# Moving 32 DRAM-to-DRAM transfers inside GpSimd's queue, and reordering the loads of one stage's entry

## The chip, the cores and the metric

The kernel runs on one core of a Trainium2 chip. The metric is device time in microseconds (us) of one execution. The engines are TensorE (PE, with its weight loads as PEld), VectorE (DVE), ScalarE (ACT) and GpSimd (POOL); SyncE (SP) only issues DMA transfers. Each engine works through its own list of instructions strictly in order, and waits at an instruction until the semaphores named there have their values. Transfers issued by SP and by GpSimd go through two queues that share the same 16 DMA engines.

## The reference

One inference step of a one-layer encoder for 544 rows (512 of a new stream, 32 of a running one), width 2048, all in fp32. The parts that matter here, cut from it:

```python
h = layer_norm(x, ln_in_g, ln_in_b)                       # x: 544 x 2048
proj = h @ w_in                                           # 2048 x 4928
hq, hf, hi, hg, cq, ckv, kr = jnp.split(proj, SPLITS, axis=-1)
o_h = hgrn2_recurrence(...)                               # 8 heads of 128
o_a = mla_attention(...)                                  # 8 heads of 128
mix = jnp.concatenate([o_h, o_a], axis=-1) @ w_out        # 2048 x 2048
h = layer_norm(ALPHA * h + mix, ln1_g, ln1_b)
ff = (silu(causal_conv3(h @ w_up)) * (h @ w_gate)) @ w_down
y = layer_norm(ALPHA * h + ff, ln2_g, ln2_b)
```

## The kernel before, in words

Activations lie transposed in SBUF: 128 features on the partitions, the 544 rows along the free axis, cut into two halves of 272 (`NI`). Every fp32 product is three matmuls: operands and weights are split into a rounded high part (`wh`, `aH`, made by ACT) and the rest (`wl`, `aL`, made by DVE as a difference), and PE multiplies high by high, low by high and high by low.

The stages, in order of time:

1. **Entry (0 to some 120 us).** SP loads the input in five row tiles (128 rows each, the fifth with the 32 rows), each as two halves, with `ident`, `par` (all small parameters) and the first eight weight blocks of 512 KB between them. For each row tile DVE takes statistics (`L277`, `L279`), GpSimd makes the factor of the norm in two tiny operations (`rs`, `L280` and `L281`, the second a power of -1/2), DVE normalises (`L287`), PE transposes (`tp`, `L297`), ACT applies the affine part and rounds (`L303`, `L304`), DVE makes the low part (`L305`). PE multiplies the first projection in `cq_half`, first for the rows of the first half, then for the second.
2. **Attention (to some 360 us).** Four pairs of heads: `proj_pair` projects and rotates a pair while `attend` works on the one before. The rotation needs the halves of each head exchanged: four SBUF copies `t<-t` on SP (`swapped`, L457 and L458), then GpSimd multiplies by the cosine (`L462`) and DVE by the sine (`L463`). `tick()` is called at every step of the projections.
3. **Recurrence (to some 790 us).** For each head two groups of weights go through a seven-product scheme (`Divided`): a 2x2 block matrix is multiplied with seven products of sums of blocks. The sums of weight blocks are made in SBUF by DVE and by accumulating transfers on GpSimd: `L782` (12 += 22, in `form`) and `L795` (11 += 21, in `low`; `form_next()` stands in the code behind it). `L994` is a tiny power on GpSimd in each head's `finish`.
4. **Block stage (790 to 945 us).** The output projection. Its first columns run with plain weights (`step`, `split_next`), and the norm's first sums are taken (`Norm.first`: `n_cb`, a copy on ACT, `L1139`). Then 28 products of the seven-product scheme (`Product`, PE `L1792`) for four column groups. Their weights come from DRAM: some are blocks of `w_out`, the others are sums of blocks. The sums of operands (`su`, tiles `us`) come from `sm_dr`, and `split_su` splits them on ACT and DVE (`L1416`, `L1417`). `out_sink` (DVE, `L1820` and `L1823`) adds a product's PSUM tile to the rows `zt`.
5. **Feed-forward and second norm (to the end).**

The **weight sums** of the block stage are the subject of the change. `forming(phase)` yields 32 transfers within DRAM on GpSimd's queue, 512 KB each, in six phases: eight plain copies of a block into its place (`wf_dr`), eight transfers that accumulate another block onto it, four copies of a sum, four accumulates, four copies, four accumulates. `form_next(n)` issues the next one if more than `n` are left. In the program text it is called from `tick()` in the attention stage, and from `low()` in the recurrence.

What sets the order: PE, DVE and ACT of the entry, and all engines of the recurrence's core and of the block stage, keep the order of the program text (`manual_schedule`). Elsewhere, for GpSimd and SP above all, a list scheduler places an instruction as early as its inputs allow by its own estimate. The weight sums have no input but DRAM weights, so it puts them at the head of GpSimd's list, among the first operations of the kernel, however late `form_next` stands in the text.

Of the kernel before, what the change touches and what calls it, by code (L numbers as in the profile page):

```python
# [11 lines left out]
ALU = mybir.AluOpType  # L12
# [47 lines left out]
def tile_encoder_step(ctx, tc, xp, xs, w_in, w_in4, w_kr, w_q_b, w_kv_b, w_out, w_out4, w_up, w_gate, w_down, w_down2,  # L60
# [33 lines left out]

    def form_next(n=0):
        if len(forms) > n:
            forms.pop(0)()

    par = const.tile([P, N_PAR], F32, name="par")
    ident = const.tile([P, P], F32, name="ident")  # L100
# [299 lines left out]
    with tc.tile_pool(name="mp", bufs=1) as mp, tc.tile_pool(name="psa", bufs=4, space=PSUM) as psa:  # L400
# [274 lines left out]

        def tick():
            ticks[0] += 1
            if ticks[0] % 7 == 0:
                form_next(12)

        weave([proj_pair(0)], [], 0.0, tick)
        weave([proj_pair(1)], [attend(0)], 2.0, tick)
        weave([proj_pair(2)], [attend(1)], 2.0, tick)
        weave([proj_pair(3)], [attend(2)], 2.0, tick)
        weave([head_ig(0)], [attend(3)], 2.0, tick)
        while len(forms) > 12:
            form_next()

    def out_piece(kk, g):
# [13 lines left out]
    with tc.tile_pool(name="gp", bufs=1) as gp, tc.tile_pool(name="psg", bufs=1, space=PSUM) as psg:  # L703
# [60 lines left out]
        class Divided:  # L764
# [26 lines left out]
            def low(self, wh):  # L791
                wl = wp.tile([P, 1024], R, name="wl", tag="wl")
                V.tensor_tensor(out=wl, in0=self.t(self.key), in1=wh.bitcast(F32), op=ALU.subtract)  # L793
                if self.name == "s2":
                    G.dma_start(self.t("11"), self.src("21"), accum_op=ALU.add)  # L795
                    form_next()
                elif self.name not in ("11", "s1"):
                    slots.append(self.raw.pop(self.key)[0])
                    supply()
                return wh, wl  # L800
# [610 lines left out]
    def load_su(n, i):  # L1411
        G.dma_start(su[n][i][:, 1].bitcast(F32), sm_dr[i][:, ("s1", "s2", "s4").index(n)])

    def split_su(n, i):
        h, l = su[n][i][:, 0], su[n][i][:, 1]
        A.activation(h, l.bitcast(F32), AF.Copy)  # L1416
        V.tensor_tensor(out=l, in0=l.bitcast(F32), in1=h.bitcast(F32), op=ALU.subtract)  # L1417
# [14 lines left out]
    def joined(k, j, ps, eng=V):  # L1432
        z = zt[k][:, H_[j]]
        V.tensor_tensor(out=z, in0=z, in1=ps, op=ALU.add)
        nrm[j].add(zt[k], eng)
# [31 lines left out]
    def step(outs, w, j, kk):  # L1467
        for t in range(2):
            for k in range(4):
                kg = CAT_ORDER[4 * kk + k]  # L1470
                mm3([(outs[t], j)], (w[0][:, kg % 4], w[1][:, kg % 4]), (t * P, t * P + P), cact(kg),
                    kk == 0 and k == 0, kk == 3 and k == 3)
# [3 lines left out]
    with tc.manual_schedule():  # L1476
        order56 = [(kk, g) for g in (5, 6) for kk in ko]
        raws56, ws56 = [], []

        def raw_next():  # L1480
            if len(raws56) < 8:
                kk, g = order56[len(raws56)]
                raws56.append(load_raw(w_out[kk, g - 4], 4, 256))

        def split_next():
            ws56.append(split_w(raws56[len(ws56)], 4, 256))
            raw_next()

        for _ in range(3):
            raw_next()  # L1490
        for k in (0, 1, 2, 4, 6):
            G.dma_start(zt[k], h0_dr[k])
        for k in (10, 11, 12, 13, 8):
            dma(zt[k], h0_dr[k])
        for k in (3, 5, 7):
            G.dma_start(zt[k], h0_dr[k])
        for n in ("s1", "s2"):
            for i in range(2):
                load_su(n, i)
        split_next()  # L1500
        split_next()
        firsts = []
        for j in range(2):
            for t in range(2):
                z = zt[t][:, H_[j]]
                V.scalar_tensor_tensor(out=z, in0=z, scalar=ALPHA, in1=wo_tiles[t][:, PS_[j]], op0=ALU.mult, op1=ALU.add)
            firsts.append(nrm[j].first(zt[0], zt[1], early[0][:, 512 * j:512 * j + 512]))
            next(firsts[j])

        def next_firsts():  # L1510
            for f in firsts:
                next(f, None)

        five, six = pair_half(early[1], 0), pair_half(main_tile(), 0)
        step(five, ws56[0], 0, 0)
        split_next()
        next_firsts()
        step(five, ws56[1], 0, 1)
        split_next()
        next_firsts()  # L1520
        for i in range(2):
            load_su("s4", i)
        step(five, ws56[2], 0, 2)
        next_firsts()
        split_next()
        shifted(10, 0)
        shifted(11, 0)
        step(five, ws56[3], 0, 3)
        split_next()
        for k in range(HK):  # L1530
            load_21(k, d3_dr[k // 2][:, k % 2])
        step(six, ws56[4], 0, 0)
        split_next()
        for t in range(2):
            joined(10 + t, 0, five[t], G)
        step(six, ws56[5], 0, 1)
        split_next()
        shifted(12, 0)
        shifted(13, 0)
# [255 lines left out]
    with tc.manual_schedule():  # L1795
# [59 lines left out]
        def restore():  # L1855
            for k in range(HK):
                load_21(k, cat_dr[4 + k // 2][:, k % 2, NI:])

        NO = len(oitems)
        ohooks = {0: [lambda: split_su("s1", 1)], 1: [lambda: split_su("s2", 0)], 2: [lambda: split_su("s2", 1)],  # L1860
                  3: [lambda: split_su("s4", 0)], 4: [lambda: split_su("s4", 1)], 5: [lambda: split_21(range(4))],
                  6: [lambda: split_21(range(4, 8))],
                  NO - 2: [lambda: split_seventh(0)],
# [5 lines left out]
        oitems[0].prep()  # L1869
        step(six, ws56[7], 0, 3)  # L1870
        oitems[1].prep()
        split_su("s1", 0)
        for t in range(2):
            joined(12 + t, 0, six[t], G)
        play(oitems, 0, ohooks)
        restore()
        for n in (2, 3):
# [756 lines left out]
```

## Time and profile before

| | us |
|---|---|
| median of 3 runs | 2414.26 (2410.18 to 2414.37) |
| profiled execution | 2413.28 |
| its span | 2410.8 |
| PE busy | 2301.5 (95% of the span) |
| DVE busy | 1716.4 (71%) |
| ACT busy | 1096.8 (45%) |
| GpSimd busy | 272.6 (11%) |

The page also has the span in 40 equal slices of 60 us, the busy share in tenths. The first two slices differ from all others:

```profile
PE   2499999999999999999999999999999999999997
PEclk8699999999999999999999999999999999999998
```

In the time lines each row gives the start in us, the duration, engine, line, operation, output and inputs with their shapes, and in brackets the time the engine had stood idle and what released it. A name like `wf3s<-in_w_out` is output and input; buffer numbers are left out. "issue" as a releaser means that the profile shows nothing that was waited for.

### The profile page before, as it was taken

How to read it: one execution, taken by the hardware profiler on the slowest of the kernel's cores; microseconds unless marked ns; L12 is line 12 of the kernel's file. 1: busy time of each engine (PE TensorE's matmuls, PEld its weight loads, DVE VectorE, ACT ScalarE, POOL GpSimd, SP SyncE). 2: the span in 40 equal slices, each digit the busy share in tenths (PEclk: the TensorE clock that was granted, in tenths of full speed). 3: DMA queues.
4: the chain of work that ended last, by engine and by line, in shares of the span. 5: the costliest groups of instructions: out<-in, count | busy, mean ns of one | idle time of the engine just before them, and what ended most of it. 6: DMA issues, size and time to landing. Idle time of an engine off the chain costs nothing.

```text
span 2410.8 us, 44619 instructions
## 1 busy us (share of the span) xinstructions
PE 2301.5 (95%) x18244; PEld 2284.0 (95%) x18244; DVE 1716.4 (71%) x2395; ACT 1096.8 (45%) x1686; POOL 272.6 (11%) x343
## 2 busy tenths in 40 slices
PE   2499999999999999999999999999999999999997
PEld 1499999999999899999999999999999999999996
DVE  2344657777767578897777777777777777777776
ACT  2144543433445345665555555555555433333323
POOL 2201100100000211010100001010000111111102
PEclk8699999999999999999999999999999999999998
DMA  9753226555556854668677677767677998889832
GB/s 288 174 135 104 91 71 201 160 138 128 134 133 194 289 173 160 224 172 263 169 220 192 183 213 181 223 167 227 183 192 206 343 333 286 263 287 306 288 104 76
DMA packets 175772, 474.55 MB, mean 197 GB/s; under 512 B 16080, under 2 KB 80336, under 8 KB 168144
## 3 DMA queue, kind: packets, MB, share of 16 engines
q1 hardware_dynamic: 140112, 316.57, 38.3%
q0 software_dynamic: 35456, 155.14, 27.8%
q8 instruction: 143, 2.34, 0.4%
q14 instruction: 61, 0.50, 0.1%
HBM read 394.36 MB, written 91.34 MB: 201 GB/s over the span
## 4 chain that ended last, share of the span: by engine, by line
PE 89%; issue 4%; DMA 2%; DVE 2%; ACT 2%; POOL 1%; SPq 0%; ACTq 0%; DVEq 0%; POOLq 0%
PE main L1312 21%; PE acc L1312 16%; PE main L850 10%; PE main L1343 10%; PE main L146 10%; PE acc L1343 7%; PE acc L146 3%; PE main L1792 2%; PE s L915 2%; PE acc L1792 2%; PE main L591 1%; PE at L652 1%; PE at L621 1%; DMA raw<-in_w_in 1%; DMA wf1s<-wf1s 0%
## 5 line engine op out<-in xcount | busy, mean ns | idle before, releaser
L1254 DVE TENSOR_TENSOR wl<-raw,wh 128x1024 fp32r<-128x1024 f32 x371 | 456.1, 1229 | 195.2 <-ACT wh L1253 194.9
L1253 ACT ACTIVATE wh<-raw 128x1024 fp32r<-128x1024 f32 x371 | 391.9, 1059 | 408.0 <-PE main L1312 98.7
L1312 PE MATMUL main<-op,wh 128*128 128x272 f32 x1408 | 265.4, 287 | 0.0
L1312 PE MATMUL acc<-ops,wh 128*128 128x272 f32 x1344 | 254.1, 287 | 0.0
L1312 PE MATMUL main<-ops,wh 128*128 128x272 f32 x1344 | 254.1, 287 | 0.0
L1312 PEld LDWEIGHTS main<-op,wh 128*128 128x128 f32 x1408 | 221.0, 188 | 0.0
L1312 PEld LDWEIGHTS acc<-ops,wh 128*128 128x128 f32 x1344 | 211.1, 188 | 0.0
L1312 PEld LDWEIGHTS main<-ops,wh 128*128 128x128 f32 x1344 | 211.0, 188 | 0.0
L1312 PE MATMUL main<-op,wl 128*128 128x272 f32 x704 | 202.9, 288 | 0.3 <-DVE wl L1254 0.3
L1312 PE MATMUL main<-ops,wl 128*128 128x272 f32 x672 | 193.7, 288 | 0.0
L1312 PE MATMUL acc<-ops,wl 128*128 128x272 f32 x672 | 193.7, 288 | 0.0
L146 PE MATMUL main<-aL,wh 128*128 128x272 f32 (+2 forms) x608 | 148.1, 295 | 36.5 <-DVE aL L305 36.5
L1312 PE MATMUL acc<-op,wh 128*128 128x272 f32 x832 | 157.5, 288 | 1.0 <-DVE eg L1617 1.0
L146 PE MATMUL main<-aH,wl 128*128 128x272 f32 (+2 forms) x608 | 149.0, 295 | 3.3 <-DVE wl L317 3.3
L1253 ACT ACTIVATE wh<-rawl 128x1024 fp32r<-128x1024 f32 x93 | 98.8, 1063 | 116.5 <-PE acc L1312 43.8
L146 PE MATMUL main<-aH,wh 128*128 128x272 f32 (+2 forms) x608 | 150.8, 299 | 0.4 <-ACT wh L316 0.4
L146 PEld LDWEIGHTS main<-aL,wh 128*128 128x128 f32 x608 | 106.1, 194 | 37.2 <-DVE aL L305 37.1
L1312 PEld LDWEIGHTS main<-op,wl 128*128 128x128 f32 x704 | 132.2, 188 | 0.5 <-DVE wl L1254 0.5
L1254 DVE TENSOR_TENSOR wl<-rawl,wh 128x1024 fp32r<-128x1024 f32 x93 | 113.8, 1223 | 25.6 <-ACT wh L1253 25.4
L1312 PEld LDWEIGHTS acc<-op,wh 128*128 128x128 f32 x832 | 130.4, 188 | 1.2 <-ACT eg L1644 1.2
L793 DVE TENSOR_TENSOR wl<-raw,wh 128x1024 fp32r<-128x1024 f32 x84 | 103.1, 1227 | 35.9 <-ACT wh L788 35.0
L1312 PEld LDWEIGHTS main<-ops,wl 128*128 128x128 f32 x672 | 126.2, 188 | 0.0
(494 smaller groups left out, 6121.0 us busy)
## 6 DMA issues: line engine op xcount, KB each, us to landing
raw<-in_w_in SPq DMA_DIRECT2D x76, 512.0 KB, 3.8
raw<-in_w_up SPq DMA_DIRECT2D x71, 512.0 KB, 5.3
raw<-in_w_gate SPq DMA_DIRECT2D x71, 512.0 KB, 4.8
raw<-in_w_down SPq DMA_DIRECT2D x67, 512.0 KB, 9.1
opd<-ohl SPq DMA_DIRECT2D x20, 1088.0 KB, 5.5
ops<-opd POOLq DMA_DIRECT2D x20, 1088.0 KB, 11.7
raw<-in_w_up POOLq DMA_DIRECT2D x35, 512.0 KB, 5.3
opd<-ohl SPq DMA_DIRECT2D x20, 816.0 KB, 6.3
```

Of the source, the lines that this page charges most:

```text
L146: PE.matmul(ps, ww[:, wcols[0]:wcols[1]], aa[:, hs[j]], start=first and i == 0, stop=last and i == 2, skip_group_check=True)
L591: PE.matmul(ps[:, j * 512:j * 512 + 256], l[k][:, a:b], r4(w[:, k:k + 1, :])[:, 0, :, 128:256], start=k == 0 and i == 0, stop=k == 1 and i ...
L621: PE.matmul(sc[:, :nk], qn[j][:, q0:q0 + P], kn[j][:, :nk], start=True, stop=False)
L652: PE.matmul(po[:, :P], vt[:, k, j, :], t[:, k * P:(k + 1) * P], start=k == 0, stop=k == b)
L793: V.tensor_tensor(out=wl, in0=self.t(self.key), in1=wh.bitcast(F32), op=ALU.subtract)
L850: PE.matmul(out, ww[:, k * P:(k + 1) * P], aa, start=name in ("11", "s1", "12") and k == 0 and q == 0, stop=k == HK - 1 and q == 2, skip_g ...
L915: PE.matmul(ps[:, j * 64:(j + 1) * 64], Kp[:, a:b], Qv[:, j * bt:(j + 1) * bt, 1, :], start=True, stop=True)
L1253: A.activation(wh, src, AF.Copy)
L1254: V.tensor_tensor(out=wl, in0=src, in1=wh.bitcast(F32), op=ALU.subtract)
L1312: PE.matmul(ps, ww[:, k * P:(k + 1) * P], aa, start=self.first and k == 0 and i == 0, stop=k == n - 1 and i == 2, skip_group_check=True)
L1343: PE.matmul(banks[:, 512 * u:512 * u + NI], ww[:, (u * n + k) * P:(u * n + k + 1) * P], aa, start=self.first and k == 0 and i == 0, stop=k ...
L1792: PE.matmul(self.bank, ww[:, k * P:(k + 1) * P], aa, start=self.first and k == 0 and i == 0, stop=k == HK - 1 and i == 2, skip_group_check ...
```

## The change

Four edits.

- `form_next` passes each of the 32 transfers to `keep_in_program_order`, which ties an instruction behind the one that stands before it on its engine in the program text. The scheduler can then no longer move it ahead. The calls are spread anew: in the attention stage one at every fourth step while more than 16 are left (before: every seventh, 12), the others in the recurrence behind `L795`, two in each group while more than eight are left, then one.
- In the block stage's entry the first two weight splits, each of which asks for the next weights, stand ahead of the row loads.
- The loads of operand sums (`load_su`) and of three rows move back: `s1` to where `s4` was, `s2`, the three rows and `s4` behind the first row products.
- The split of the first sum `s1` moves from ahead of the products into the first product's hook. The two rows 12 and 13 are added on DVE as before, but their squares and sums for the norm become fill-in work between the products.

```diff
     def form_next(n=0):
         if len(forms) > n:
-            forms.pop(0)()
+            tc.keep_in_program_order(forms.pop(0)())
...
         def tick():
             ticks[0] += 1
-            if ticks[0] % 7 == 0:
-                form_next(12)
+            if ticks[0] % 4 == 0:
+                form_next(16)
...
-        while len(forms) > 12:
+        while len(forms) > 16:
             form_next()
...
                 if self.name == "s2":
                     G.dma_start(self.t("11"), self.src("21"), accum_op=ALU.add)
-                    form_next()
+                    for _ in range(2 if len(forms) > 8 else 1):
+                        form_next()
...
         for _ in range(3):
             raw_next()
+        split_next()
+        split_next()
         for k in (0, 1, 2, 4, 6):
             G.dma_start(zt[k], h0_dr[k])
         for k in (10, 11, 12, 13, 8):
             dma(zt[k], h0_dr[k])
-        for k in (3, 5, 7):
-            G.dma_start(zt[k], h0_dr[k])
-        for n in ("s1", "s2"):
-            for i in range(2):
-                load_su(n, i)
-        split_next()
-        split_next()
...
         for i in range(2):
-            load_su("s4", i)
+            load_su("s1", i)
         step(five, ws56[2], 0, 2)
...
         for t in range(2):
             joined(10 + t, 0, five[t], G)
+        for i in range(2):
+            load_su("s2", i)
+        for k in (3, 5, 7):
+            G.dma_start(zt[k], h0_dr[k])
+        for i in range(2):
+            load_su("s4", i)
         step(six, ws56[5], 0, 1)
...
-        ohooks = {0: [lambda: split_su("s1", 1)], 1: [lambda: split_su("s2", 0)], 2: [lambda: split_su("s2", 1)],
+        ohooks = {0: [lambda: split_su("s1", 0), lambda: split_su("s1", 1)], 1: [lambda: split_su("s2", 0)], 2: [lambda: split_su("s2", 1)],
...
         oitems[1].prep()
-        split_su("s1", 0)
         for t in range(2):
-            joined(12 + t, 0, six[t], G)
+            V.tensor_tensor(out=zt[12 + t][:, H_[0]], in0=zt[12 + t][:, H_[0]], in1=six[t], op=ALU.add)
+            fill(0.8, lambda t=t: nrm[0].add(zt[12 + t], G))
```

How the instructions move, at three places, GpSimd's in two stretches. The first is GpSimd's list in the entry, around the third pair of `rs` operations (the 32-row tile). Before (`wf3s`, `wf4s` and so on are the weight sums in DRAM; 16x8192 is a plain copy, 256x512 an accumulate):

```order
L91 DMA wf3s_107<-in_w_out 256x512
L91 DMA wf3s_109<-in_w_out 256x512
L280 TENSOR_SCALAR rs<-mv 32x1
L91 DMA wf4s_111<-in_w_out 256x512
L281 TENSOR_TENSOR rs<-rs,nhalf 32x1
L91 DMA wf4s_113<-in_w_out 256x512
L91 DMA wf1s_100<-wf1s_99 16x8192
L91 DMA wf2s_104<-wf2s_103 16x8192
```

Now, from the input's first clearing on:

```order
L253 MEMSET x_137 128x2048
L280 ISA
L280 TENSOR_SCALAR rs<-mv 128x1
L281 TENSOR_TENSOR rs<-rs,nhalf 128x1
L280 TENSOR_SCALAR rs<-mv 128x1
L281 TENSOR_TENSOR rs<-rs,nhalf 128x1
L280 TENSOR_SCALAR rs<-mv 32x1
L281 TENSOR_TENSOR rs<-rs,nhalf 32x1
```

All 32 transfers have left this part of the list. Where half of them went: GpSimd's list in the recurrence, behind each group's `L795` (`L995` is the power that was `L994`):

```order
L795 DMA raw<-in_w_in 128x1024
L91 DMA wf1s_100<-in_w_out 256x512
L91 DMA wf2s_104<-in_w_out 256x512
L995 TENSOR_TENSOR r_5203<-r_5202,nhalf 128x5
L782 DMA raw<-in_w_in 128x1024
L795 DMA raw<-in_w_in 128x1024
L91 DMA wf3s_108<-in_w_out 256x512
L91 DMA wf4s_112<-in_w_out 256x512
L782 DMA raw<-in_w_in 128x1024
```

Before, `L782`, `L795` and `L994` stood there alone. The second place is SP's list at the block stage's entry (`raw` and `xr` are weights, `sm` a store of operand sums, `zb` rows). Before:

```order
L125 DMA raw<-in_w_out 128x1024 x4
L976 DMA out_sts<-s1o 128x128
L971 DMA out_stp<-S 128x128
L1019 DMA sm_98<-sm 384x1x272
L1494 DMA zb<-h0d_79 128x544
L1494 DMA zb<-h0d_80 128x544
L1494 DMA zb<-h0d_81 128x544
L1494 DMA zb<-h0d_82 128x544
L1494 DMA zb<-h0d_77 128x544
L125 DMA raw<-in_w_out 128x1024 x3
L1241 DMA xr_8713<-in_w_out 128x1024
```

Now:

```order
L125 DMA raw<-in_w_out 128x1024 x4
L977 DMA out_sts<-s1o 128x128
L125 DMA raw<-in_w_out 128x1024
L972 DMA out_stp<-S 128x128
L125 DMA raw<-in_w_out 128x1024
L1020 DMA sm_98<-sm 384x1x272
L1497 DMA zb<-h0d_79 128x544
L1497 DMA zb<-h0d_80 128x544
L1497 DMA zb<-h0d_81 128x544
L1497 DMA zb<-h0d_82 128x544
L1497 DMA zb<-h0d_77 128x544
```

Two weight loads now stand ahead of the store and of the rows, where they stood behind them. The third is DVE's list from the addition of rows 12 and 13 to the first product's sink. Before:

```order
L1417 TENSOR_TENSOR us_8414<-us_8414 128x1088
L1434 TENSOR_TENSOR zb<-zb,main 128x272
L1161 TENSOR_TENSOR n_s_8544<-n_s_8544,n_e 128x272
L1434 TENSOR_TENSOR zb<-zb,main 128x272
L1161 TENSOR_TENSOR n_s_8544<-n_s_8544,n_e 128x272
L1254 TENSOR_TENSOR wl<-raw_8717,wh 128x1024
L1417 TENSOR_TENSOR us_8415<-us_8415 128x1088
L1823 SCALAR_TENSOR_TENSOR za<-za,main 128x272
```

Now:

```order
L1875 TENSOR_TENSOR zb<-zb,main 128x272 x2
L1255 TENSOR_TENSOR wl<-raw_8717,wh 128x1024
L1418 TENSOR_TENSOR us_8414<-us_8414 128x1088
L1418 TENSOR_TENSOR us_8415<-us_8415 128x1088
L1162 TENSOR_TENSOR n_s_8537<-n_s_8537,n_e 128x272 x2
L1825 SCALAR_TENSOR_TENSOR za<-za,main 128x272
```

The first split of `s1` (`us_8414`) now stands behind the row additions, and the squares (`n_s`) behind both splits.

## The prediction

> **What bounds the kernel now.** I read the busy time by stretch first, then the waits of the first 130 us, then the time lines of the engines those waits name. The columns of the first view are the stretch, its length, busy us (instructions) of PE, PEld, DVE, ACT and POOL, the granted PE clock, the DMA share and GB/s.
>
> ```profile
> 0.00:20.00 20.00, 0.00 (x0) 0.00 (x0) 4.58 (x12) 1.74 (x3) 6.02 (x13) 1.00 0.91 331
> 20.00:60.00 40.00, 12.48 (x73) 11.36 (x73) 11.77 (x23) 16.31 (x31) 7.02 (x9) 0.79 0.94 268
> 60.00:120.00 60.00, 27.66 (x172) 26.73 (x173) 21.92 (x35) 10.76 (x23) 15.09 (x22) 0.66 0.73 173
> 120.00:215.00 95.00, 94.80 (x754) 94.61 (x753) 40.42 (x65) 35.42 (x59) 7.71 (x9) 1.00 0.48 128
> 215.00:335.00 120.00, 118.56 (x872) 111.21 (x871) 72.89 (x208) 64.52 (x149) 15.59 (x23) 1.00 0.30 91
> 800.00:845.00 45.00, 38.96 (x297) 38.37 (x295) 28.82 (x43) 20.15 (x27) 7.95 (x12) 0.96 0.88 318
> ```
>
> PE is full from 120 us on, apart from about 6 us of the block stage's entry (800 to 845). Of the first 120 us it works 40, so 80 us are idle there, and nothing in that stage is PE's own limit. The waits of 0 to 130 us (us in total, times, longest):
>
> ```profile
> PE tp L297 <- DVE x L287: 39.6, 3, 22.1
> PE main L146 <- DVE aL L305: 36.5, 2, 34.6
> DVE x L287 <- POOL rs L281: 57.5, 4, 35.4
> ```
>
> PE waits for DVE, and DVE for two tiny GpSimd operations per row tile (`rs`, the factor of the input norm). GpSimd's time line, 37 to 71 us, says why they are late (last column: idle before, and what ended it):
>
> ```profile
> 37.67 0.92 POOL L91 DMA_DIRECT2D wf1s<-in_w_out  x1 [10.54 <-issue]
> ...
> 64.87 0.59 POOL L280 TENSOR_SCALAR rs<-mv 32x1 f32<-32x1 f32 x1
> 69.80 0.95 POOL L91 DMA_DIRECT2D wf4s<-in_w_out  x1 [4.34 <-issue]
> 70.43 0.93 POOL L281 TENSOR_TENSOR rs<-rs,nhalf 32x1 f32<-32x1 f32 x1
> ```
>
> Two operations of under 1 us (after the mean of row tile 4, ready at 36.0) stand in order behind accumulating transfers of weight sums (L91), each of which goes out 4 to 11 us after the one ahead of it. So the first 120 us are bound by GpSimd's queue, not by arithmetic.
>
> **The change, part one: the 32 transfers leave the head of GpSimd's queue.** In the changed order the five pairs of `rs` operations follow each other with no L91 between. What DVE did at the waits:
>
> ```profile
> 5.04 2.52 DVE L277 BATCH_NORM_STATS2 st<-x 128x6 f32<-128x512 f32 x4 [4.13 <-DMA x<-in_xp]
> 25.48 0.55 DVE L287 TENSOR_SCALAR x<-x,mv,rs 128x512 f32<-128x512 f32 x1 [1.26 <-POOL rs L281]
> 35.76 0.25 DVE L279 BATCH_NORM_AGGREGATE mv<-st 32x2 f32<-32x24 f32 x1
> 71.40 1.33 DVE L287 TENSOR_SCALAR x<-x,mv,rs 32x2048 f32<-32x2048 f32 x1 [35.39 <-POOL rs L281]
> 72.66 1.41 DVE L305 TENSOR_TENSOR aL<-x,aH 128x256 fp32r<-128x256 f32 x4
> 74.00 2.34 DVE L317 TENSOR_TENSOR wl<-raw,wh 128x1024 fp32r<-128x1024 f32 x2
> 76.27 2.45 DVE L277 BATCH_NORM_STATS2 st<-x 128x6 f32<-128x512 f32 x4
> 111.11 1.35 DVE L287 TENSOR_SCALAR x<-x,mv,rs 128x2048 f32<-128x2048 f32 x1 [16.05 <-POOL rs L281]
> 112.51 0.69 PE L297 MATMUL tp<-ident,x 128*128 128x128 f32 x2 [14.01 <-DVE x L287]
> ```
>
> *From 36 to 112.5 us.* DVE's mean of the 32-row tile is ready at 36.0. With `rs` at once (0.59 + 0.93) DVE normalises at 37.6 and then has, in its order up to the transposes at 112.51: normalise 1.33; aL 1.41, wl 2.34, statistics 2.45 + 0.25; aL, wl, statistics once more (6.45); normalise 1.35; aL 1.41, wl 2.34; normalise 1.35. Together 20.7 us, so the transposes can start at 58.3 instead of 112.5: **-54 us**. PE's part of that stretch fits: about 120 matmuls at 0.12 us and 16 transposes of 0.13, some 16 us.
>
> *The start.* Ahead of the first matmul stand two row tiles of 1 MB each, `ident`, `par` and the first weights, all on SP's queue (the first row is GpSimd's queue up to 130 us: packets, MB, share of the 16 engines):
>
> ```profile
> q0 software_dynamic: 4214, 15.55, 50.6%
> par<-in_par SPq DMA_DIRECT2D x1, 239.0 KB, 15.2
> 19.75 1.06 ACT L316 ACTIVATE wh<-raw 128x1024 fp32r<-128x1024 f32 x1 [0.83 <-DMA raw<-in_w_in]
> ```
>
> The first half tile is there at 5.04: 0.52 MB at the 331 GB/s of the first row is 1.6 us, so 3.4 us go by before data flows. Up to `par` it is 2.41 MB, which alone on the engines is there at 3.4 + 7.3 = 10.7; the first weights (2.93 MB) at 12.3 instead of 19.7. Statistics of half a tile (1.3), mean (0.25), `rs` (1.2) and normalise (0.55) end about 14.0, where 25.48 + 0.55 = 26.0 stands now: **-12 us**.
>
> *The clock.* The granted clock is 0.66 in the mean of 60 to 120 us; after each long stop PE starts at the low one:
>
> ```profile
> 97.10 0.41 PE L146 MATMUL main<-aL,wh 128*128 128x256 f32 x1
> 97.31 0.36 PE L146 MATMUL main<-aH,wl 128*128 128x256 f32 x1
> 97.62 0.28 PE L146 MATMUL main<-aL,wh 128*128 128x256 f32 x1
> 97.74 0.28 PE L146 MATMUL main<-aH,wl 128*128 128x256 f32 x1
> ```
>
> A matmul follows the one before it by 0.21 us at the low clock and by 0.12 at the full one (97.10 to 97.31, 97.62 to 97.74). 24 of them cost 2 us behind 112.5 (the earlier stop's are inside the -54): **-2 us**. Against this I set **+2 us** for waits that come up once everything is packed: ACT delivers aH as fast as DVE takes it, and DVE then works 38 of some 45 us. Part one: -66. Bounds: -71 if those waits don't come and the first tiles land 3 us sooner; -56 if SP's loads of the entry (8 half tiles, 8 weight blocks of 512 KB and the small ones, 9.0 MB) flow at the 268 GB/s of the second row, 3.4 + 33.4 = 37 us instead of 30, so that the last weights make PE some 6 us late, and the start gains 8 instead of 12.
>
> **Part two: where the 32 transfers go.** Sixteen go into the attention stage, the others behind each group's own accumulate (L795) in the recurrence stage.
>
> ```profile
> t<-t SPq DMA_DIRECT2D x15, 68.0 KB, 2.1
> h0d<-x SPq DMA_DIRECT2D x16, 128.0 KB, 8.8
>   DMA t<-t: 0.3, 1
> 546.24 0.88 POOL L782 DMA_DIRECT2D raw<-in_w_in  x1 [21.79 <-DVE raw L780]
> 569.90 1.19 POOL L994 TENSOR_TENSOR r<-r,nhalf 128x5 f32<-128x5 f32 x1 [16.39 <-DVE r L993]
> ```
>
> In attention (215 to 335 us) the DMA share is 0.30, GpSimd is busy 15.6 of 120 us and PE full. The tender spot is the rotation of the query: four small SBUF copies (`t<-t`, 2.1 us each to land; first row) whose end DVE's L463 awaits, without slack: once it waited 0.3 us already (third row); the softmax is queued behind it on DVE, and PE behind that. Small SP transfers took 8.8 us beside the weight sums at the start (second row). So the cost is between 0 and 4 pairs x 6.7 = 27 us. GpSimd's new order puts the copies of the second pair well ahead of its rotation and one transfer each near those of the third and fourth, so I take the end near 0: **+3 us**, with 1 us in it for two accumulates ahead of the memsets before the recurrence. In the recurrence GpSimd stands idle for 22 us behind an L795 until L782, and for 16 ahead of L994 (last rows); two accumulates need 0.9 + 5 + 0.9, so **0**. Above zero only if they held the queue for 16 us, for which even the longest step at the start (10.5 idle, 0.9 issue) and an issue are too short.
>
> The Trainium skill's page "SBUF — State Buffer" (SBUF: two separate sides) speaks against this move: it says that a GpSimd transfer's descriptors can't be written while DVE runs an operation that uses both ports, and its section "A bandwidth-pool intuition that's wrong" has 620 ns growing to 3100. DVE is 61% busy in attention, and by that rule 16 issues grow by some 2.2 us each there, 35 us of GpSimd's time by estimate, in a stage where 104 of 120 are free. The rows here disagree in size: beside a busy DVE the recurrence's issue at 546 takes 0.88 us. By rule or row the sum is the same.
>
> **Part three: the block stage's entry.** Two stalls, seen on ACT, PE and DVE:
>
> ```profile
> 801.05 3.62 SPq L125 DMA_DIRECT2D raw<-in_w_out  x3
> 810.00 1.06 ACT L134 ACTIVATE wh<-raw 128x1024 fp32r<-128x1024 f32 x1 [13.46 <-DMA raw<-in_w_out]
> 811.39 0.84 PE L1125 MATMUL acc<-ident,nt_c 128*128 128x128 f32 x6 [2.00 <-ACT n_cb L1139]
> 830.38 0.28 PE L1792 MATMUL main<-aL,wh 128*128 128x272 f32 x1
> 836.30 0.43 DVE L1823 SCALAR_TENSOR_TENSOR za<-za,main 128x272 f32<-128x272 f32 x1
> 836.87 0.36 PE L1792 MATMUL main<-aH,wh 128*128 128x272 f32 x1 [3.45 <-ACT us L1416]
> ```
>
> The first: ACT sits 13.5 us on weights that SP asked for at 801, behind row loads and a store; the centre's copy (`n_cb`) queues behind it and PE waits 2.0. Now SP asks before the store and the rows, so `n_cb` comes when PE is done; PE's 0.84 us of spreading follows at once: -1.6 us. The second, 3.45 us, is put down to ACT, but PE restarts 0.57 us after DVE's L1823, which reads the PSUM tile that the next product shares. In the changed order five operations still stand between the row additions and that L1823: one weight split, two splits of sums, two additions of squares (before: the same but one split of sums). Starting when PE has gone on from the row products, at 830.4 (third row): 0.8 + 1.2 + 2.5 + 1.3 = 5.8 us, against 836.3 - 830.4 = 5.9 now. So this stall stays, and only -0.4 comes from loads that are less crowded. Part three: **-2 us**, between 0 and -7.5 (both stalls and 2 us of half clock gone).
>
> **Sum.** The profiled execution took 2413.28 us (span 2410.8, 2.5 around it): 2413.3 - 66 - 2 + 3 = **2348 us**. It is 1.0 below the median of the runs shown (2414.26), less than their own spread (2410.18 to 2414.37).
>
> **Rivals.**
> *The traffic comes back in attention.* For it: L463 has no slack, and 8.8 us beside 2.1. Against it: the copies of one pair are out before its rotation. At 6.7 us for each of four pairs: 2348 + 24 = 2372; at half, 2360.
> *The entry becomes bound by its loads.* For it: the DMA share there is 0.91 to 0.94. Against it: the weight sums leave, which had half of the engines' time in the first 130 us (the queue row ahead of `par`). At -56: 2358.
> *The block entry opens altogether.* For it: the wait is named as ACT's, which the moved split relieves. Against it: the DVE row above. At -7.5: 2342.
> *Slower than before: accumulates hold GpSimd in the recurrence.* Each accumulate issues only when the one before has left room; if in the recurrence two of them held L782 and L994 past their 16 to 22 us, every one of the 12 groups would pay. The loss passes the gain of 65 from 5.4 us in each group on, that is from about 25 us for two accumulates; at 8 us each it would be 2348 + 96 = 2444. For it: steps up to 11.5 us at the start. Against it: those ran beside SP's loads at a share of 0.94, and here L782 and L994 wait for DVE alone.
> *It doesn't do what it says*, GpSimd's order staying as it was: 2413. The order shows it is not so; no chance.
>
> **How the numbers follow.** Forecast 0.62 (2348), traffic in attention 0.15 (2360 to 2372), loads 0.12 (2358), block entry open 0.08 (2342), slower 0.03. The range reaches from 2337 (part one at -71, block at -7.5) to 2366 (loads, or half the traffic and a little more); some 0.15 lies outside. About 0.2% (5 us) is what a measurement of this kernel can tell from no change. Faster by more than that holds in all cases but the last: 0.96; within it 0.01; slower 0.03.
>
> **What would show it.** Right: the first matmul near 15 us, the transposes of the second half near 46 (58 less the 12 of the start), no DVE wait on `rs` above 2 us, the granted clock at 1.0 from about 20 us on; L463 and L782 where they were relative to PE's work; a PE wait of about 3 us still there on the block stage's second product. Wrong: a DVE wait on `t<-t` of several us in attention, a PE wait on `aL` or `wl` released by DMA in the entry, L782 late behind L91, or a block entry with no wait at all.

## The result and the profile after

| | before | after |
|---|---|---|
| median (range; runs) | 2412.28 (2410.18 to 2414.37; 4) | 2353.30 (2351.54 to 2357.51; 4) |
| profiled execution | 2413.28 | 2357.51 |
| its span | 2410.8 | 2355.7 |

The ratio is 0.9758, with a 95% interval from 0.9741 to 0.9776: 59.0 us faster. The forecast was 2348, with a range from 2337 to 2366. The profiled execution of the changed kernel is the slowest of its four, so the profiles show a gain of 55, not 59.

The busy time by stretch, columns as before:

```profile
0.00:20.00 20.00, 7.44 (x40) 6.51 (x41) 12.91 (x30) 7.32 (x14) 4.06 (x9) 1.00 0.90 322
20.00:60.00 40.00, 37.08 (x291) 36.33 (x290) 29.77 (x49) 29.36 (x58) 3.41 (x6) 0.96 0.61 204
60.00:120.00 60.00, 59.80 (x475) 59.61 (x474) 24.95 (x39) 18.27 (x31) 3.64 (x5) 1.00 0.34 102
215.00:335.00 120.00, 114.53 (x833) 109.24 (x833) 62.17 (x172) 45.25 (x100) 15.92 (x19) 0.94 0.56 146
```

PE works 104 of the first 120 us instead of 40, and the clock is at 0.96 to 1.00 there. The last row shows what was lost: from 215 to 335 us PE stands 5.5 us (1.4 in the same stretch before, which holds other work), and the clock is 0.94 (1.00 before). The entry's waits (us in total, times, longest), and behind them the time line at three points of its chain:

```profile
PE tp L297 <- DVE x L287: 12.6, 2, 9.6
DVE x L287 <- POOL rs L281: 1.8, 2, 1.0
PE main L146 <- DVE wl L317: 1.8, 1, 1.8
PE main L146 <- DVE aL L305: 1.0, 1, 1.0
```

```profile
14.66 0.58 PE L146 MATMUL main<-aH,wh 128*128 128x256 f32 x1
22.77 0.25 DVE L279 BATCH_NORM_AGGREGATE mv<-st 32x2 f32<-32x24 f32 x1
44.33 1.47 PE L297 MATMUL tp<-ident,x 128*128 128x128 f32 x12
```

The wait for `rs` fell from 57.5 us to 1.8. The first matmul comes at 14.7, the mean of the 32-row tile at 23.0 (36.0 before), the second half's transposes at 44.3 (112.5 before).

PE's order is the same in both kernels, so the start of one and the same PE instruction in the two traces tells how much has been gained up to there. This ledger is worked out from the two profiled executions (56 us apart); a minus is a gain:

| place in the changed kernel (us) | forecast | measured |
|---|---|---|
| entry, to 120 | -66 | -70.6 |
| third pair's rotation, 206 | } +2 | +1.2 |
| fourth pair's rotation, 242, and half clock behind it | } | +2.5 +1.7 |
| ahead of the recurrence, 317, and half clock behind it | +1 | +2.5 +4.7 |
| recurrence, with its last loads, 715 | 0 | +1.8 |
| block entry, first stall, 754 | -1.6 | -1.5 |
| block entry, second stall, 780, and half clock behind it | -0.4 | +0.4 +1.2 |
| from there to the end | 0 | +1.0 |
| sum | -65 | -55.1 |

The two places that cost most, in the time lines of the changed kernel (and, from before, in the third list, the rows that answer to the last two):

```profile
227.93 0.94 POOL L91 DMA_DIRECT2D wf1s<-in_w_out  x1
238.67 0.72 DVE L463 TENSOR_TENSOR t<-t,sin 128x544 f32<-128x544 f32 x1 [3.59 <-DMA t<-t]
241.66 0.44 PE L638 MATMUL at<-ident,p 128*128 128x128 f32 x2 [2.41 <-DVE o L653]
```

```profile
303.06 0.87 POOL L91 DMA_DIRECT2D wf4s<-in_w_out  x1
312.01 0.89 POOL L91 DMA_DIRECT2D wf4s<-in_w_out  x1 [8.09 <-DMA s<-h0d]
312.57 1.39 POOL L708 MEMSET attnT<- 128x544 f32 x2
313.10 0.44 DVE L181 TENSOR_TENSOR s_f<-s,s 128x272 f32<-128x272 f32 x1 [4.76 <-DMA s<-h0d]
317.48 1.54 PE L916 MATMUL s<-Qp,Kp 128*128 128x64 f32 x8 [3.00 <-DVE Kp L922]
328.62 0.35 PE L919 MATMUL s<-Qp,Kp 128*128 128x16 f32 x2
```

```profile
380.27 1.11 PE L915 MATMUL s<-Qp,Kp 128*128 128x64 f32 x8 [0.48 <-DVE Kp L921]
386.72 0.35 PE L918 MATMUL s<-Qp,Kp 128*128 128x16 f32 x2
```

The gain is 62.8 us at the first of these pairs (380.27 - 317.48) and 58.1 at the second (386.72 - 328.62). Between them PE is never idle: it runs at half clock, for some 10 us behind a stop of 3.0. At the fourth pair an accumulate went out 3 us ahead of the four small copies `t<-t`; they landed 6.4 us after their issue instead of 2.1 (both medians of the list of transfers), and DVE waited 3.6 us. The rows of the lists are `t<-t` at the fourth pair and `s<-h0d` ahead of the recurrence, changed kernel, and `s<-h0d` at that place before; the last row is the stretch behind the stop of 3.0 us (columns as above):

```profile
t<-t SPq DMA_DIRECT2D x4, 68.0 KB, 6.4
s<-h0d SPq DMA_DIRECT2D x11, 136.0 KB, 5.3
s<-h0d SPq DMA_DIRECT2D x14, 136.0 KB, 3.4
317.40:328.40 11.00, 10.92 (x53) 10.92 (x53) 6.23 (x16) 1.92 (x3) 0.00 (x0) 0.53 0.97 303
```

Ahead of the recurrence two things come late at once, the rows of `h0d` (L181) and the clearing of `attnT` (L708, behind an accumulate that itself waited 8 us). The first of the two clearings ends at 313.5, when DVE is done with L181. At the block stage's entry:

```profile
753.65 0.84 PE L1126 MATMUL acc<-ident,nt_c 128*128 128x128 f32 x6 [0.53 <-ACT n_cb L1140]
775.14 3.06 DVE L1418 TENSOR_TENSOR us<-us 128x1088 fp32r<-128x1088 f32 x2
778.12 0.98 DVE L1162 TENSOR_TENSOR n_s<-n_s,n_e 128x272 f32<-128x272 f32 x2
779.02 0.43 DVE L1825 SCALAR_TENSOR_TENSOR za<-za,main 128x272 f32<-128x272 f32 x1
779.59 0.56 PE L1794 MATMUL main<-aH,wh 128*128 128x272 f32 x1 [3.83 <-DVE za L1825]
```

The first stall is 0.5 us instead of 2.0. The second is still there, and the profile now names DVE's sink for it, where it named ACT before.

### The profile page after: what moved, and what is told of

Same layout as the page of the kernel before. It is cut to its first block, busy times and chain, and to the rows that moved or that the text cites. A ratio compares the mean times of both kernels' runs of the same rounds, so it can differ in the third digit from the quotient of the medians.

```text
span 2355.7 us, 44621 instructions
## 1 busy us (share of the span) xinstructions
PE 2304.0 (98%) x18244; PEld 2285.7 (97%) x18244; DVE 1714.7 (73%) x2395; ACT 1095.9 (47%) x1686; POOL 273.9 (12%) x343
## 4 chain that ended last, share of the span: by engine, by line
PE 90%; DVE 3%; DMA 3%; ACT 2%; issue 1%; POOL 0%; SPq 0%; ACTq 0%; DVEq 0%; POOLq 0%
PE main L1313 21%; PE acc L1313 16%; PE main L1344 10%; PE main L146 10%; PE main L851 10%; PE acc L1344 7%; PE acc L146 3%; PE main L1794 2%; PE s L916 2%; PE acc L1794 2%; PE main L591 1%; PE at L652 1%; DMA cx<-catd 1%; PE at L621 1%; DMA x<-in_xp 1%
## 5 line engine op out<-in xcount | busy, mean ns | idle before, releaser
L1313 PEld LDWEIGHTS acc<-ops,wl 128*128 128x128 f32 x672 | 126.4, 188 | 0.8 <-DVE wl L1255 0.8
```

The lines of the kernel that those rows point to most:

```text
L1313: PE.matmul(ps, ww[:, k * P:(k + 1) * P], aa, start=self.first and k == 0 and i == 0, stop=k == n - 1 and i == 2, skip_group_check=True)
```

## The experiments

Each run was timed beside the kernel before on the same chip; ratios are to that kernel, with their 95% intervals. Gains "at" a place are read from the start of the same PE instruction, as in the ledger.

### What held the entry: the queue or the bytes

`e3_copies_early`: the accumulates become plain copies, in the order of before.

```diff
-                yield lambda out=f[out], src=src, add=add: G.dma_start(out, src, **({"accum_op": ALU.add, "max_dma_last_dim": 2048} if add else {}))
+                yield lambda out=f[out], src=src, add=add: G.dma_start(out, src)
```

> The kernel before, with its order, but the 16 accumulating transfers of the weight sums replaced by plain copies of the same blocks to the same places (so the sums aren't formed, and the block stage multiplies with wrong weights; as much work). Theory A, the queue: accumulates go out 4 to 11 us apart and hold the rs operations behind them, copies don't, so rs comes soon, and only the traffic remains: with half of the engines' time gone, 9 MB of loads need some 55 us instead of 30, the second half's transposes start near 60 to 70 instead of 112.5, and the whole takes 2360 to 2372. Theory B, the traffic: it is the bytes beside the input's loads that make the entry late, wherever they stand; as many bytes, so 2405 or more, transposes beyond 105.

Measured: 2376.89, ratio 0.9849 (0.9836 to 0.9862). From its time lines and waits:

```profile
38.38 0.59 POOL L281 TENSOR_TENSOR rs<-rs,nhalf 32x1 f32<-32x1 f32 x1
64.70 1.06 ACT L316 ACTIVATE wh<-raw 128x1024 fp32r<-128x1024 f32 x1 [10.31 <-DMA raw<-in_w_in]
71.53 1.47 PE L297 MATMUL tp<-ident,x 128*128 128x128 f32 x12
```

The factor of the 32-row tile comes at 38 us instead of 70, the second half's transposes at 71.5 instead of 112.5. Of the 68 us that the changed kernel gains up to there, 41 come back though all transfers stay early, as theory A has it. The other 27 are put down to the bytes (here ACT waits 10 us for weights, and the DMA share is 1.01 to 1.02 from 20 to 85 us), which is more than the estimate had: the whole took 5 us more than its range. The edit takes away two things at once, the adding and the small pieces (16 rows of 32 KB instead of 256 of 2 KB), and this run can't tell which of them holds the queue.

`e11_ring`: the kernel before, one number changed.

```diff
-nc = bacc.Bacc("TRN2", target_bir_lowering=False, num_devices=1, dynamic_dma_scratch_size=1024)
+nc = bacc.Bacc("TRN2", target_bir_lowering=False, num_devices=1, dynamic_dma_scratch_size=2048)
```

> The kernel before with twice the room for GpSimd's descriptors (the program's scratch for them 2048 instead of 1024). If an accumulate goes out only when the one ahead has left room, a second one now goes out with it, the rs pairs come up one or two accumulates sooner each, and the second half's transposes start at 85 to 105 instead of 112.5: 2385 to 2405. If the step between accumulates is set by something else: 2410 to 2415.

Measured: 2381.06, ratio 0.9867 (0.9851 to 0.9883). From its time lines:

```profile
26.19 1.94 POOL L91 DMA_DIRECT2D wf1s<-in_w_out  x2
27.39 1.65 POOL L91 DMA_DIRECT2D wf2s<-in_w_out  x1
37.10 0.89 POOL L91 DMA_DIRECT2D wf2s<-in_w_out  x1 [8.06 <-issue]
50.77 0.93 POOL L281 TENSOR_TENSOR rs<-rs,nhalf 32x1 f32<-32x1 f32 x1
77.82 2.40 PE L297 MATMUL tp<-ident,x 128*128 128x128 f32 x10 [4.72 <-DMA raw<-in_w_in]
```

Three accumulates now go out one behind the other before one waits; `rs` is there at 51 us instead of 70, and 32 us are gained, more than expected. So the "issue" waits of the accumulates are for room for their descriptors, and this room held the entry: it accounts for 35 of the 68 us at the transposes, which now wait for weights.

`e12_tie_only`: the tie without the new spread.

```diff
-            forms.pop(0)()
+            tc.keep_in_program_order(forms.pop(0)())
```

> The kernel before with the tie alone: the 32 transfers keep their place in the program's text, but the calls stand as before (every seventh step of the attention stage, the rest of the first twenty at its end, one in each recurrence group). Eight accumulates and four copies then stand in one row on GpSimd ahead of the clearing of attnT. Theory A (each accumulate waits for the one ahead to leave room, some 8 us each, and what stands behind them waits): the entry is as fast as the changed kernel's, but the clearing comes some 60 to 75 us late and PE stands that long ahead of the recurrence: 2400 to 2420, the gain nearly gone. Rival (a held GpSimd is hidden there, or the accumulates go out faster without the entry's loads): one stall of 5 to 20 us, 2350 to 2365.

Measured: 2385.76, ratio 0.9885 (0.9868 to 0.9903). GpSimd's time line, and the waits from 290 to 380 us:

```profile
300.63 0.95 POOL L91 DMA_DIRECT2D wf1s<-in_w_out  x1
351.42 0.90 POOL L91 DMA_DIRECT2D wf4s<-in_w_out  x1 [5.00 <-issue]
353.94 1.40 POOL L708 MEMSET attnT<- 128x544 f32 x2
```

```profile
DVE attnT L899 <- POOL attnT L708: 32.2, 1, 32.2
PE s L915 <- DVE attnT L931: 27.3, 1, 27.3
```

The entry gains its 70 us, and 40 of them are lost ahead of the recurrence: the row of accumulates only moved to another place where something waits behind it. Neither expected range was met; the size of theory A was overestimated: the eight go out between 300.6 and 351.4 us, 7.3 us apart in the mean, and PE has work for some of that time. So the tie alone is worth 28 us, about half of the change; the rest of the way to 2353.3 comes with the spread of the calls.

### What the moved transfers cost

`e7_no_sums`: no transfers at all.

```diff
-    forms = [f for phase in range(6) for f in forming(phase)]
+    forms = []
...
-            src = wf_dr[g, name] if (g, name) in wf_dr else out_block(g, {"11": "11", "12": "21", "s4": "22"}[name])
+            src = out_block(g, {"12": "21", "s4": "22", "22": "22", "s3": "12"}.get(name, "11"))
```

> The changed kernel without the 32 transfers; the block stage's products that need a sum load a plain block of the output weights instead (so its products are wrong, as many bytes to load). It prices all that the moved transfers cost: by the ledger of the traces 12 us up to the recurrence's start and 1.2 at its end, so 2338 to 2342, no wait on t<-t above 0.7 us, no stall ahead of the recurrence nor of cx at its end. By the forecast's term (3 us) 2350.

Measured: 2342.39, ratio 0.9707 (0.9694 to 0.9721). The stalls of the ledger from 206 to 715 us are gone (the one ahead of the recurrence is 0.03 us; one wait of 0.8 us on `t<-t` is left), the two of the block entry stay. So the transfers cost the changed kernel 11 us in the medians, 14 in the ledger; the forecast said 3.

`e4_calm`: only the eight first copies in the attention stage, the rest two by two in the recurrence.

```diff
-                form_next(16)
+                form_next(24)
...
-        while len(forms) > 16:
+        while len(forms) > 24:
...
-                    for _ in range(2 if len(forms) > 8 else 1):
+                    for _ in range(2):
```

> The changed kernel with only the eight plain copies in the attention stage, and the 16 accumulates and 8 later copies in the recurrence, two behind each L795. Theory A: the changed kernel lost 12 us between PE's 206 and 330 us to accumulates, which make small transfers land late beside them (t<-t at the fourth pair, h0d rows and the memsets ahead of the recurrence), and the recurrence hides two of them in each group; so no wait on t<-t above 1 us, no stall of 3 us ahead of the recurrence, and 2341 to 2345. Rival, the slower case of the forecast: two accumulates hold GpSimd past L782 or the power L995 in the four groups that have them now and had one, 3 to 6 us each: 2353 to 2365. Rival C: the stalls come from the packed stage itself, and stay: 2353.

Measured: 2349.44, ratio 0.9736 (0.9723 to 0.9750).

```profile
  DMA t<-t: 1.2, 1
```

```profile
705.09 0.49 PE L146 MATMUL main<-aH,wh 128*128 128x272 f32 x2 [1.47 <-ACT wh L134]
706.93 0.47 PE L952 MATMUL sw<-ident,Kp 128*128 128x128 f32 x1 [1.11 <-DVE Kp L922]
```

The first row, of the view of L463, is what DVE waits there for `t<-t` (4.2 us in the changed kernel; 1 at most was expected); the others are of PE's time line. At the fourth pair the same store and weight load of SP stand beside the four copies as in the changed kernel, and without the accumulate they land in 2.1 us (3.1 in `e7_no_sums`). Up to 328 us this kernel is 10.4 us ahead of the changed one, as theory A said, and it holds that up to 700 us with two accumulates in every group: the rival of the held GpSimd does not show. Then 4.5 us go at a place that no theory had named: accumulates issued at 677 and 688 lie beside the loads at the recurrence's end, whose weights now come late. So the time lies 4 us above theory A's range.

`e6_memset_first`: the last accumulate of the attention stage behind the clearing.

```diff
-        while len(forms) > 16:
-            form_next()
...
         G.memset(kT[:, 4], 0.0)
+        while len(forms) > 16:
+            form_next()
```

> The changed kernel with the last accumulate of the attention stage issued behind the clearing of attnT and kT instead of ahead of it. Theory M: that accumulate, which goes out only when the one before it has landed, holds the clearings, and they make the 3.0 us stall ahead of the recurrence; the stall falls under 1 us, with the half clock behind it gone 6 us less: 2346 to 2349. Theory L: the rows of h0d land late beside the accumulates (5.8 us each, 4.0 before), and DVE's first sum waits for them as long; the stall stays at 2.5 us or more, 2351 to 2354.

Measured: 2355.91, ratio 0.9763 (0.9748 to 0.9778). From its time lines:

```profile
308.84 1.04 POOL L706 MEMSET attnT<- 128x544 f32 x2 [2.89 <-DMA d3d<-o]
315.27 0.44 DVE L181 TENSOR_TENSOR s_f<-s,s 128x272 f32<-128x272 f32 x1 [3.78 <-DMA s<-h0d]
319.59 1.77 PE L916 MATMUL s<-Qp,Kp 128*128 128x64 f32 x8 [3.08 <-DVE Kp L922]
```

The clearing is now done more than 5 us before it is used, and the stall is 3.1 us all the same: theory L, the rows of `h0d` land late beside an accumulate, and that is enough for the stall. Whether the late clearing alone would make one too, no run here tests.

### The block stage's entry

`e1_forms_only` and `e2_block_only`: the four edits of the change, split in two (the edits of `form_next`, `tick` and `low` alone; the edits of the block stage alone).

> The kernel before with the weight sums' edits alone (the tie to the program's order and the new spread), the block stage's entry as it was. If the ledger of the two traces is right, the block stage's edits take 1.5 us off its first stall and give about as much back at its second one (3.45 before, 3.83 after, and half clock behind it), so this kernel takes what the changed one takes, 2353, within 2 us. If the block's edits are worth the 2 us of the forecast, it takes 2355; if they opened the entry, about 2360.

> The kernel before with the block stage's edits alone, the weight sums where they were. By the ledger 2412 to 2413, no change; by the forecast's term 2410; if the entry opened, 2405. In all cases PE still waits some 3.5 us on the second product of the block stage, by my theory for DVE's sink of the first one.

Measured: 2358.61, ratio 0.9768 (0.9753 to 0.9783), and 2412.37, ratio 0.9995 (0.9986 to 1.0004). The intervals can't tell the block stage's edits from nothing; in the profiles they are worth 1.0 and 1.3 us, and PE waits 4.2 and 3.8 us on the second product. By its median `e1_forms_only` lies 5.3 us above the changed kernel, outside the 2 us that were expected; the two were not timed beside each other, and by the ratios it is 2.4 us.

`e5_banks`: the second product to the other PSUM tile.

```diff
-oitems = [out_item(g, "11", X[g]) for g in range(1, 5)]
+oitems = [out_item(g, "11", X[g]) for g in (1, 3, 2, 4)]
```

> The changed kernel with the block stage's first four products in the order of the groups 1, 3, 2, 4, so that the second product goes to the other PSUM tile. Theory A, the shared tile: PE waits 3.8 us at the second product because DVE's sink of the first one has not read the same tile; now the second product follows at once, and the third (which shares the first one's tile) waits 1 us at most; with the half clock behind the stall gone, 4 us less than the changed kernel: 2347 to 2350. Theory B, the operands: PE waits for the splits of the first sum on ACT, as the profile of before named it; the stall of 3.8 us stays: 2353.

Measured: 2349.09, ratio 0.9733 (0.9720 to 0.9747). DVE's time line, and PE's waits from 765 to 800 us:

```profile
773.96 3.06 DVE L1418 TENSOR_TENSOR us<-us 128x1088 fp32r<-128x1088 f32 x2
777.83 0.43 DVE L1825 SCALAR_TENSOR_TENSOR za<-za,main 128x272 f32<-128x272 f32 x1
```

```profile
PE main L1794 <- DVE za L1825: 0.8, 1, 0.8
```

The splits and the sink stand where they were, and PE waits 0.8 us, at the third product, which shares the first one's tile. So it was the tile, not the operands, though the profile of before had named ACT.

### A version without these stalls

`e8_spread` joins three edits to the changed kernel: the product order of `e5_banks`, the first copies at every second step (`ticks[0] % 2`, `form_next(24)`), and the recurrence's share by a list.

```diff
-                    for _ in range(2 if len(forms) > 8 else 1):
+                    for _ in range(share.pop(0)):
...
+        share = [2, 2, 2, 2, 4, 2, 2, 4, 2, 2, 0, 0]
```

> The changed kernel with three edits: the eight first copies on every second step of the attention stage, so that none lies beside the third pair's rotation; the other 24 in the recurrence as 2, 2, 2, 2, 4, 2, 2, 4, 2, 2, 0, 0 for its twelve groups (the fours are plain copies), so that none lies beside the loads at its end; and the block stage's first products in the order 1, 3, 2, 4. If small transfers beside an accumulate are the whole cost: no wait on t<-t above 0.7, none of the stalls at the recurrence's two ends, none at the second product: 2336 to 2341. If four copies or two accumulates in a group hold GpSimd or the weights' loads: 2345 to 2350.

Measured: 2335.06 (2334.18 to 2341.94), ratio 0.9678 (0.9665 to 0.9691): 18 us faster than the changed kernel. Its profile is of its slowest execution:

```profile
152.30 0.55 POOL L91 DMA_DIRECT2D wf2s<-in_w_out  x1
162.91 0.48 PE L623 MATMUL at<-krh,qr 128*128 128x128 f32 x1 [2.57 <-DMA qr<-low]
```

`e9_early_copies` moves the copies away from `qr`, `e10_late_copies` puts all eight into the recurrence's first group (both edits against `e8_spread`):

```diff
-            if ticks[0] % 2 == 0:
+            for _ in range({2: 1, 3: 1, 4: 2, 8: 1, 12: 1, 16: 1, 20: 1}.get(ticks[0], 0)):
                 form_next(24)
```

```diff
-            if ticks[0] % 2 == 0:
-                form_next(24)
+            pass
...
-        while len(forms) > 24:
-            form_next()
...
-        share = [2, 2, 2, 2, 4, 2, 2, 4, 2, 2, 0, 0]
+        share = [8, 2, 2, 2, 2, 4, 2, 2, 4, 2, 2, 0]
```

> The kernel of the spread (first product order 1, 3, 2, 4; recurrence 2, 2, 2, 2, 4, 2, 2, 4, 2, 2, 0, 0), with the eight copies of the attention stage placed so that none is asked for within 6 us ahead of a small transfer: four in the gap before the first pair's rotation, two behind that pair's query rows, two behind the second pair's. The spread's trace had one copy 0.9 us ahead of the query rows (qr) and four right behind them; the second row transfer took 8.9 us instead of 2.3, PE waited 2.6 us and lost 3 more at half clock. If that is all that is left: no PE wait above 1 us from 50 to 800 us, 2331 to 2336 (the spread: 2335). If four copies at once make the weights late in the first gap: 2336 to 2341.

> The same with all eight copies in the recurrence's first group, and the other 24 one group later each (8, 2, 2, 2, 2, 4, 2, 2, 4, 2, 2, 0), so that the attention stage has none. If only small transfers beside the bulk ones cost: 2331 to 2336, attention as without the sums. If eight copies at once (some 25 us of the engines) hold the recurrence's weight loads, or two accumulates in the last but one group reach the loads at its end: stalls there of 2 us or more, 2338 to 2343.

Measured: 2335.24 (2334.42 to 2336.96), ratio 0.9675 (0.9662 to 0.9689), and 2341.60, ratio 0.9701 (0.9687 to 0.9715). The longest PE wait of the first from 50 to 800 us, and the stall of the second:

```profile
PE main L1795 <- DVE za L1826: 0.8, 1, 0.8
```

```profile
393.47 1.06 ACT L786 ACTIVATE wh<-raw 128x1024 fp32r<-128x1024 f32 x1 [6.59 <-DMA raw<-in_w_in]
397.53 0.36 PE L849 MATMUL main<-aH,wh 128*128 128x272 f32 x1 [2.83 <-DVE hproj L837]
```

The first has no wait of 1 us left in that stretch. Its median is that of `e8_spread` all the same, so the `qr` stall of that profile is shown for that execution alone. Eight copies at once make the recurrence's weights late, as the second expectation had it.

## Why the prediction was right, and where its sizes were off

**What bounds the kernel: right.** GpSimd's queue, and in it the room for accumulates' descriptors, held the entry. `e3_copies_early` and `e11_ring` show both without moving a transfer, and `e12_tie_only` gains the whole entry with the tie alone.

**Part one, -66: -70.6.** The start is 13 us earlier (forecast 12), the chain from the mean of the 32-row tile to the transposes takes 21.3 us (22.3), the clock gives its 2. The +2 for waits of the packed entry is what failed: PE's new waits (1.8 and 1.0 us) lie inside the chain that was already counted. The marks named for this part came out: first matmul at 14.7 (near 15), transposes at 44.3 (near 46), no wait for `rs` above 1 us. The clock is the exception: it falls to 0.50 once more from 28 to 31 us, behind PE's new waits. The rival of an entry bound by its loads needed those 9 MB to last 37 us; in the changed kernel the DMA engines are done with them at some 31.

**Part two, +3: the mis-sized term, 11 by the medians, 14 by the ledger.** Its bounds (0 to 27) held the size; the choice near the lower end failed, and with it the sentence that set 1 us for two accumulates ahead of the memsets. That place cost 7.2, and taking the memsets out of it gained nothing (`e6_memset_first`): rows of `h0d` that land late suffice for the stall, a transfer which the working did not list among the tender spots. The named one, `t<-t`, cost 5.4 at two pairs, so the first rival was half right in its mechanism, and the time lies between the forecast and it. A sign of being wrong that the prediction named, a DVE wait on `t<-t` of several us, came true there (3.6 us). The prediction's price of 6.7 us a pair came from stores of 128 KB; the four copies landed 4.3 us late. Also left out was the half clock behind each stop, 6.4 us in all, as much as the stops of attention themselves (6.2). In the recurrence the 0 holds but for the last loads (+1.8), though two accumulates took longer than the forecast had it: from 439.8 to 450.3 us and from 466.0 to 478.2, and `L782` and `L995` still wait for DVE alone behind them. The L91 issues of attention take 0.49 to 0.94 us. The Trainium skill's page "SBUF — State Buffer" (A bandwidth-pool intuition that's wrong) would have each grow by some 2.2 us beside a busy DVE, by the estimate on record, which counts all of DVE's busy time though the page's figure is for a `tensor_copy`. No run here shows such a growth, and the measurement decides. The small transfers landed in 6.4 us instead of 2.1 beside an accumulate of the other queue. The Trainium skill's page "DMA: Bandwidth & Descriptors" (Queues, rings and completion order) has each engine take turns between its queues, a whole packet at a time. The late landings agree with it in kind; the turns themselves no run here shows.

**Part three, -2: about 0 by the ledger, not to be told from nothing by the medians.** Both mechanisms were right: the first stall lost 1.5 (forecast 1.6), the second stayed for the reason given, DVE's queue ahead of the sink and the shared tile (`e5_banks`). The loads that were to be less crowded gave nothing (+0.4), and half clock behind the stall took 1.2.

**The slower rival** had the right mechanism in the wrong place. Two accumulates in a group hold nothing in the recurrence (`e4_calm`); eight in a row where PE waits soon cost some 40 us (`e12_tie_only`).

That the sum came out as near as 5 us is in part luck: an entry 4.6 us better than forecast made up for part of a traffic term 8 to 11 us too low.

## What to carry to other kernels

A transfer without inputs may float to the head of its queue; look there first when tiny operations on that engine come late, and when it is moved, give it a place where no small, awaited transfer is in flight, on either queue, not just a place where its own engine is idle. Price a short stop of PE together with the half clock behind it, and give that price a range (see below). Where the profile names one releaser of several, change that one thing (here the PSUM tile) before believing it.

## What was not expected of the hardware

- Doubling the room for GpSimd's descriptors took 32 us off the kernel before (2413.54 to 2381.06), with no instruction moved.
- One 512 KB transfer on GpSimd's queue made small ones of SP land late: `t<-t` (68 KB) 6.4 us instead of 2.1, `h0d` rows (136 KB) 5.3 instead of 3.4 (medians of the lists of transfers).
- Behind a stop of 3.0 us the granted clock was 0.53 for the next 11 us (317.4 to 328.4), which cost 4.7 us, more than the stop. The length of the stop does not set it: behind a stop of 3.0 us at the same place in `e5_banks` the clock was back at 1.00 after some 7 us, and behind the single stops of 2.1 to 4.4 us in the profiles of this case it lasted 3.4, 6.8 or 10.2 us where it came. So a microsecond or more between two executions of one kernel may be this alone.
